# FFN up projection of a streaming encoder step: cache store, operand addresses, sample rounds and the order of the first pass

## The chip, the cores and the metric

The kernel runs on one core of one Trainium2 chip. The metric is the device time of one execution in microseconds (us). Three runs of the kernel before gave 1390.81, 1395.69 and 1397.09 us; the median, 1395.69 us, is its time. A further execution was profiled, and the profile is read from that one.

## The reference, cut to what matters

One layer: a mixer, a residual, then a feed-forward block whose up-projected rows go through a causal convolution of width 3 before the gated product.

```python
def conv_ffn(xn, buf, w_up, conv_w, conv_b, w_down):
    up = xn @ w_up                                   # (T, 1024) @ (1024, 5632)
    up, buf = causal_dwconv(up, buf, conv_w, conv_b) # buf: last 2 up-projected rows
    gate, val = jnp.split(up, 2, axis=-1)
    return (jax.nn.gelu(gate, approximate=True) * val) @ w_down, buf
...
x = x + rms_norm(h, g_mix_post[l])
h, ffn_buf = conv_ffn(rms_norm(x, g_ffn_pre[l]), ...)
x = x + rms_norm(h, g_ffn_post[l])
```

It is computed for a prompt of 1024 rows and for 32 sample rows that continue another stream. `ffn_buf`, the last two up-projected rows (2 x 5632 values), is an output for each of the two: `p_fc` and `q_fc`, both laid out 128 x 44 x 2.

## The kernel before, in words

The mixer and its output projection come first. `outproj` (L1074 on) handles units of 128 rows, 0 to 7, and unit 8, the sample rows: product with `w_out` (tiles zp), norm, residual, second norm, then eight transposes (tiles fxt, L1194) into features-first form. Units 0 to 4 and 8 are stored to `xn_d` and read back; units 5, 6 and 7 are written straight into the tiles x0 and xg1 (L1197 on ScalarE for unit 5, L1199 on VectorE for 6 and 7). Unit 7's norm is a chain over four engines: squares (L1159, ScalarE), sum and power (L1163, L208, L209, GpSimd), scaling (L1167, L1168, VectorE), squares (L1175), L208, L209, scaling (L1178), transposes, L1199.

**FFN up.** The product with `w_up` goes by Strassen-Winograd: seven products of quarter size in place of eight (p1 to p7). The output features are taken in NF = 22 blocks, `up_block` (L1309 on), each a pair of 128 gate and 128 value features. The moving operands are made once from the normed x by `col_operands` (L1227 on): B21, B11, T1, B22 and T2, T4, T3, each as a high and a low half of the fp32 value, so that one product of fp32 values is three matmuls (`mm3`, L88, L89, L90: high by high, high by low, low by high). Products p6, p4 and p7 use T2, T4 and T3. The stationary operands (A and S tiles) are halves of the block's weights, made by `up_operands`; the weights of block f + 1 are loaded (L1276, tiles wu) on SyncE's queue while block f runs. A block is 84 matmuls of 128x512.

Block 0 is cut in two, s = 0 and s = 1, each on 256 columns of every half of the prompt, because units 6 and 7 come late. In block 0, T2, T4 and T3 of s = 0 go into a pool px1 that lies where the output projection's weights lie until their last matmul. In `up_block` the bank of p6 is copied away (c6, L1329, ScalarE) before p7 adds to it.

**Order of the work.** The program is written as generators that are stepped by hand; a scheduler then fixes one static order for each engine, by emission order, priorities (`tc.high_priority`) and ordering hints (`tc.issue_after`). Each engine takes its instructions strictly in that order, and so does each queue: an instruction that waits holds all behind it. SyncE's queue carries the weight loads, the stores of finished blocks (h_d, L1407) and the sample weights.

**Sample rows.** `up_samples` (L1413 on) multiplies the 32 sample rows by `w_up` in fp32 in 24 rounds, (g, k) for three column groups and eight slices of 128 rows; each round uses one 1 MB buffer of two, and reloads it (L1418). `up_all` steps this generator between the two halves of a block. At its end the last two columns of `smp_u` are stored to `q_fc`: for each of 128 partitions 44 pieces of two values, 8 bytes each, from a row of 34 values.

**FFN down** (`down_all`) is also seven products (P2, P1, P4, P6, P5, P7, P3), each 11 steps of 12 matmuls, 132. Its stationary operands are halves of h (tag hop) in a pool ph that takes over the place of px0 (B21, B11, T1, B22); its moving operands are weight halves in p4.

**Addresses.** A pool lays its tiles end to end. By the tiles' sizes, B21, B11, T1, B22 and all weight halves in p4 start on multiples of 64 bytes. T2, T4 and T3 start 32 bytes past one, and so do h's halves (behind a 32-byte tile `pad` in ph). The output projection's two operands, both in p2, start 32 bytes past one as well.

Of the kernel before, what the change touches and what calls it, by code (L numbers as in the profile page):

```python
# [8 lines left out]
F32 = mybir.dt.float32  # L9
# [10 lines left out]
DEC = 32  # L20
# [58 lines left out]
def body(ctx: ExitStack, tc: tile.TileContext, a: dict):  # L79
# [988 lines left out]
    def outproj(p2, W, u):  # L1068
# [113 lines left out]
        if u < 5 or u == 8:  # L1182

            zt = z[:, :8 * n].rearrange("p (k n) -> p k n", n=n)
        else:
            s = u > 5
            o = 128 * (u - 4) - 256 * s
            zt = xlate[s][:, :, o:o + n]
        for hf in range(2):
            p, t, b = (upper[0], "xw", 4) if u == 5 else (upper[0], *(("xw", 4), ("sx", 1))[hf]) if 5 < u < 8 else (psb, "big", 3)  # L1190
            ps = p.tile([128, 4, 128], F32, tag=t, name=f"fxt{u}{hf}", bufs=b)
            for k in range(4):
                c = 512 * hf + 128 * k
                pe.transpose(ps[:, k, :n], z[:n, c:c + 128], ident[:n, :n])  # L1194
# [32 lines left out]
    def col_operands(pool_, q, s, between=lambda: None, res=None, only=False, c=slice(None), stages=(0, 1), begun=()):  # L1227

        res = {} if res is None else res
        q = {k: v[:, :, c] for k, v in q.items()}  # L1230
        at = slice(256 * s + (c.start or 0), 256 * s + (c.stop or 256))

        def halves(name, src):
            if name not in res:
                p = pool_[name in ("T2", "T4", "T3")]
                res[name] = tuple(p.tile([128, 4, 512], F32R, name=f"{name}{x}") for x in "hl")
            h, l = (t[:, :, at] for t in res[name])
            with ExitStack() as late:
                if s == 0 and name in ("B21", "B11"):
                    late.enter_context(tc.issue_after(kept["ch"].ins))  # L1240
                    late.enter_context(tc.issue_after(kept["cl"].ins))
                act.copy(h, src)
                return dve.tensor_tensor(l, src, h.bitcast(F32), op=ALU.subtract)

        if not begun:
            halves("B21", q["B21"])
            halves("B11", q["B11"])
        if only:
            return res
        t1 = q["B11"]  # L1250
        if 0 in stages:
            between()
            dve.tensor_tensor(t1, q["B12"], t1, op=ALU.subtract)
            halves("T1", t1)
            halves("B22", q["B22"])
        if 1 not in stages:
            return res
        t3, t2, t4 = q["B12"], q["B22"], q["B21"]
        dve.tensor_tensor(t3, q["B22"], t3, op=ALU.subtract)
        dve.tensor_tensor(t2, t2, t1, op=ALU.subtract)  # L1260
        dve.tensor_tensor(t4, t2, t4, op=ALU.subtract)
        with ExitStack() as behind:
            if s == 0:
                behind.enter_context(tc.issue_after(kept["jk"].ins))
            halves("T2", t2)
        ins = halves("T4", t4)
        between()
        with tc.issue_after(ins.ins):
            halves("T3", t3)
        return res  # L1270
# [45 lines left out]
    def up_block(pw_, f, s, W, X, uu, own={}):  # L1316
# [21 lines left out]

        y = bank(psb, "big", "puy", 3)
# [5 lines left out]
        if f == NF - 1:  # L1345
            prod(w, "p5", True, True)
            c5 = keep("c5", w)
            prod(x, "p1", True, True)
            c1 = keep("c1", x)
            out(0, 0, c1, y)  # L1350
            prod(w, "p3", False, True)
            yield
            prod(x, "p6", False, True)
            c6 = keep("c6", x)
            prod(z, "p4", True, True)
        elif f:
            prod(x, "p1", True, True)
            c1 = keep("c1", x)
            out(0, 0, c1, y)
            prod(w, "p5", True, True)  # L1360
            c5 = keep("c5", w)
            prod(z, "p4", True, True)
            yield
            prod(x, "p6", False, True)
            c6 = keep("c6", x)
            prod(w, "p3", False, True)
        else:

# [12 lines left out]
            c6 = keep("c6", x)  # L1381
            prod(z, "p4", True, True)
# [26 lines left out]
    def up_samples():  # L1409
# [19 lines left out]
        for g, (c0, nq) in enumerate(UGROUPS):  # L1429
            ps = psf.tile([128, 512], F32, tag="sx", name=f"us{g}", bufs=1)  # L1430
            for k in range(8):
# [4 lines left out]
                if k < 7:  # L1436
                    yield
# [9 lines left out]
        sp.dma_start(a["q_fc"], smp_u[:, :, DEC:DEC + 2])  # L1447
# [13 lines left out]
    def up_all(pw_, W0, X, uus, py, freed, ahead, begun):  # L1461
# [5 lines left out]
        for f in range(NF):  # L1467
# [3 lines left out]
            for s in (0, 1) if f == 0 else (None,):  # L1471
# [371 lines left out]
    blk = up_block(pw_, 0, 0, W0, X, uus[0], own)  # L1843
# [9 lines left out]
    sp.dma_start(fconv, a["fconv"])  # L1853
    uus[0] += [p7.tile([128, 2 + SEQ], F32, name=f"uu{j}") for j in range(2)]
# [14 lines left out]
    with tc.high_priority(offset=10 * AHEAD):  # L1869
        col_operands(px, q1, 1, res=X, only=True)  # L1870
# [19 lines left out]
    for i, _ in enumerate(up_all(pw_, W0, X, uus, lambda: py[0], freed, ahead, blk)):  # L1890
        if i == 1:

            for x, c in zip(last, (slice(0, 128), slice(128, 256))):
                with tc.issue_after(done[0].ins), tc.issue_after(kept["c6"].ins):
                    next(x)
                col_operands(px, q1, 1, res=X, c=c, stages=(0,), begun=True)
            col_operands(px, q1, 1, res=X, stages=(1,), begun=True)
# [4 lines left out]
    sp.dma_start(a["p_fc"], fhalo)  # L1902
    p9s.close()
# [142 lines left out]
```

## Time and profile before

| | |
|---|---|
| median of three runs | 1395.69 us |
| the profiled execution | 1403.19 us |
| its span, first to last instruction | 1401.4 us |
| around the span | 1.8 us |
| mean granted TensorE clock | 0.977 |
| TensorE (PE) busy | 1324.7 us, 95% |
| VectorE (DVE) busy | 1014.0 us, 72% |
| ScalarE (ACT) busy | 693.8 us, 50% |
| GpSimd (POOL) busy | 310.5 us, 22% |

All times in the rows are microseconds from the span's start. A row of the timeline has start, duration, engine, line, operation, out<-in, partitions and elements, and in brackets the idle time before it with what ended it. A matmul's duration is modelled and overlaps the next one, so its pace is read from the distance between starts. A row of the stage table has the stretch, its length, busy time and instruction count of PE, of its weight loads, of DVE, ACT and POOL, then the granted TensorE clock (1.00 is full), the mean busy share of the 16 DMA engines and the GB/s that they moved. FFN up runs from 661 to 1160 us, FFN down from there to 1392 us.

### The profile page before, as it was taken

The numbers are of one execution on the slowest core, as the hardware profiler recorded it, in microseconds if no ns is written. First come the engines' busy times: TensorE is split into PE (matmuls) and PEld (weight loads), VectorE is DVE, ScalarE is ACT, GpSimd is POOL, SyncE is SP. The second block draws the span as 40 slices with busy tenths as digits, with TensorE's granted clock in tenths as the row PEclk, the third lists the DMA queues.
The fourth block names the chain that finished last, engine by engine and source line by source line (L and its number), as shares of the span: only waits on it lengthen the run. The fifth ranks groups of instructions, "written<-read, shape, count | busy, mean of one in ns | idle before, by whom it ended". The sixth has DMA issues, their size and how long they took to land.

```text
span 1401.4 us, 25578 instructions
## 1 busy us (share of the span) xinstructions
PE 1324.7 (95%) x9896; PEld 1103.0 (79%) x9896; DVE 1014.0 (72%) x1748; ACT 693.8 (50%) x1294; POOL 310.5 (22%) x411
## 2 busy tenths in 40 slices
PE   7999999998989999999799999999994999999997
PEld 6999899997988978687677777777773777678885
DVE  5886569768697687846887777788772965499456
ACT  5546556445665455525454444445441544444552
POOL 4533212144122442321101102123013100010005
PEclk9999999999999999989899999999997999999999
DMA  9799879776899654434257878876759339644335
GB/s 342 242 342 359 281 229 310 236 268 199 280 292 340 215 189 160 150 120 152 77 184 209 239 194 227 226 194 198 199 148 38 89 131 354 262 156 142 124 111 120
DMA packets 140288, 291.73 MB, mean 208 GB/s; under 512 B 34519, under 2 KB 69495, under 8 KB 138039
## 3 DMA queue, kind: packets, MB, share of 16 engines
q1 hardware_dynamic: 126535, 267.03, 58.8%
q0 software_dynamic: 9120, 18.62, 7.4%
q10 hardware_dynamic: 4512, 4.46, 0.9%
q8 instruction: 77, 1.26, 0.4%
q14 instruction: 44, 0.36, 0.1%
HBM read 229.38 MB, written 85.78 MB: 225 GB/s over the span
## 4 chain that ended last, share of the span: by engine, by line
PE 57%; DVE 8%; DMA 7%; ACT 3%; issue 2%; POOL 1%; SPq 0%; DVEq 0%; POOLq 0%; ACTq 0%
PE pux_None L88 4%; PE pux_None L90 4%; PE pux_None L89 4%; PE q L88 3%; PE q L89 3%; PE q L90 3%; PE puw_None L89 3%; PE puw_None L88 3%; PE puw_None L90 3%; PE x L88 2%; DMA wu19r<-in_w_up 2%; PE x L89 2%; PE x L90 2%; PE us L1433 2%; PE zp L88 1%
## 5 line engine op out<-in xcount | busy, mean ns | idle before, releaser
L1403 DVE SCALAR_TENSOR_TENSOR y<-uu,fconv_sb,y 128x1024 f32<-128x1024 f32 x88 | 116.0, 1318 | 23.3 <-ACT y L1401 22.9
L1400 POOL COPY fhalo<-uu 128x2 f32<-128x2 f32 x44 | 17.7, 402 | 369.1 <-DVE uu L1334 369.1
L88 PE MATMUL pv<-wt_0h,xh 128*128 128x256 f32 (+1 forms) x192 | 55.8, 291 | 4.2 <-DVE xl L321 1.6
L90 PE MATMUL zp<-woh,cl 128*128 128x512 f32 (+1 forms) x144 | 57.9, 402 | 1.5 <-DVE cl L1093 1.5
L88 PE MATMUL zp<-woh,ch 128*128 128x512 f32 (+1 forms) x144 | 57.7, 410 | 0.7 <-ACT ch L1092 0.7
L89 PE MATMUL zp<-wol,ch 128*128 128x512 f32 (+1 forms) x144 | 58.1, 404 | 0.0
L1401 ACT ACTIVATE y<-uu,fconv_sb 128x1024 f32<-128x1024 f32 x44 | 54.8, 1245 | 6.3 <-DVE uu L1334 5.1
L90 PE MATMUL pv<-wt_1h,xl 128*128 128x256 f32 (+1 forms) x192 | 55.4, 289 | 0.0
L88 PE MATMUL pv<-wt_1h,xh 128*128 128x256 f32 (+1 forms) x192 | 54.9, 286 | 0.0
L89 PE MATMUL pv<-wt_1l,xh 128*128 128x256 f32 (+1 forms) x192 | 54.6, 284 | 0.0
L90 PE MATMUL pv<-wt_0h,xl 128*128 128x256 f32 (+1 forms) x192 | 54.4, 283 | 0.0
L89 PE MATMUL pv<-wt_0l,xh 128*128 128x256 f32 (+1 forms) x192 | 54.2, 282 | 0.0
L1636 POOL TENSOR_TENSOR gss<-gss 128x1 f32<-128x1 f32 (+1 forms) x9 | 8.0, 887 | 194.9 <-ACT gjk L1629 194.9
L208 POOL TENSOR_SCALAR hrs<-hss 128x5 f32<-128x5 f32 (+3 forms) x27 | 11.0, 408 | 177.8 <-DVE hss L1002 174.7
L818 DVE COPY_PREDICATED P<-masks_sb,sc 128x352 f32<-128x352 int32 (+3 forms) x53 | 37.8, 713 | 5.8 <-PE sc L731 5.2
L88 PEld LDWEIGHTS pv<-wt_0h,xh 128*128 128x128 f32 x192 | 35.9, 187 | 6.1 <-DVE xl L321 1.9
L1006 POOL TENSOR_TENSOR cat<-cat,gt 128x320 f32<-128x320 f32 (+3 forms) x27 | 31.3, 1160 | 26.1 <-DVE cat L1004 25.9
L88 PEld LDWEIGHTS pv<-wt_1h,xh 128*128 128x128 f32 x192 | 36.3, 189 | 0.7 <-issue 0.6
L209 POOL TENSOR_TENSOR hrs<-hrs,mhalf 128x5 f32<-128x5 f32 (+3 forms) x27 | 36.2, 1341 | 2.2
L90 PEld LDWEIGHTS pv<-wt_1h,xl 128*128 128x128 f32 x192 | 36.3, 189 | 0.3
L89 PEld LDWEIGHTS pv<-wt_1l,xh 128*128 128x128 f32 x192 | 36.3, 189 | 0.1
L89 PEld LDWEIGHTS pv<-wt_0l,xh 128*128 128x128 f32 x192 | 35.9, 187 | 0.2
(1881 smaller groups left out, 4684.7 us busy)
## 6 DMA issues: line engine op xcount, KB each, us to landing
wus<-in_w_us SPq DMA_DIRECT2D x16, 1024.0 KB, 7.8
wrP<-in_w_dn SPq DMA_DIRECT2D x27, 512.0 KB, 3.9
h_d<-y SPq DMA_DIRECT2D x22, 512.0 KB, 4.7
ht<-h_d SPq DMA_DIRECT2D x22, 512.0 KB, 9.9
wt_0r<-in_w_tok SPq DMA_DIRECT2D x21, 512.0 KB, 5.6
wt_1r<-in_w_tok SPq DMA_DIRECT2D x21, 512.0 KB, 6.4
ws_d<-in_w_dn POOLq DMA_DIRECT2D x20, 512.0 KB, 7.4
wrP<-ws_d SPq DMA_DIRECT2D x20, 512.0 KB, 3.8
```

Source lines behind the costliest of these rows:

```text
L88: pe.matmul(ps, lh[0], rh[0], start=first, stop=False, **kw)
L89: pe.matmul(ps, lh[0], rh[1], start=False, stop=False, **kw)
L90: return pe.matmul(ps, lh[1], rh[0], start=False, stop=last, **kw)
L208: pool.tensor_scalar(out, ss, 1.0 / width, eps, op0=ALU.mult, op1=ALU.add)
L209: pool.tensor_tensor(out, out, mhalf[:n, :cols], op=ALU.pow)
L818: dve.copy_predicated(dst, mk.broadcast_to([n, 11, *mk.shape[2:]]), src)
L1006: pool.tensor_tensor(cat[:n, c0:c0 + 64 * nh], cat[:n, c0:c0 + 64 * nh], gt[:n, c0:c0 + 64 * nh], op=ALU.mult)
L1400: behind["POOL"] = pool.tensor_copy(fhalo[:, j, :], u[:, SEQ - 2:SEQ])
L1401: act.activation(y, u, AF.Identity, scale=fconv[:, j, 2:3], bias=fconv[:, j, 3:4])
L1403: dve.scalar_tensor_tensor(y, uu[i][:, s:s + SEQ], fconv[:, j, s:s + 1], y, op0=ALU.mult, op1=ALU.add)
L1433: pe.matmul(ps[DEC * q:DEC * q + DEC], smp_x[:, k, :], wus[:, i % 2, q, :], start=k == 0, stop=k == 7)
L1636: pool.tensor_tensor(ss[:n, 0:1], ss[:n, 2:3], ss[:n, 3:4], op=ALU.add)
```

## The change

- **Cache.** The two columns are first copied on GpSimd into a packed tile `fcq`, and `fcq` is stored to `q_fc` after FFN up, behind the store of `p_fc`.
- **Addresses.** Two 32-byte tiles are put around x0, `fcq` takes 352 bytes; together T2, T4 and T3 move by 416 bytes, six and a half times 64. The 32-byte `pad` in ph goes, so h's halves move by 32 bytes.
- **Sample rounds.** The generator yields after every second round, and `up_all` steps it up to 15 times where it stepped it 28; the first step, which loads the sample cache (5632 pieces of 8 bytes) and the first two buffers, comes in block 2, not 1.
- **First pass.** `col_operands` is cut into parts: B (B21, B11), T (T1, B22), t (T2, T4), q (T3). Unit 5's transposes are kept in PSUM, and its eight scalings (L1197) are issued after B11's high half. T2 and T4 of s = 0 are written into the upper, not yet used columns of B22 and T1 (`early`), ahead of px1; four GpSimd copies of 128x1024 values take them to their place later. B21 and B11 of s = 1 are issued after T3.
- **Last block.** In block 21 the order is p5, p1, p2, p3, p6, p4, p7; it was p2, p5, p1, p3, p6, p4, p7.

```diff
@@ outproj
+        held = []
...
-            if 5 <= u < 8 and (u, hf) not in ((6, 0), (6, 1), (7, 0), (7, 1)):
-                for k in range(4 * hf, 4 * hf + 4):
-                    act.activation(zt[:, k, :], ps[:, k % 4, :], AF.Copy, scale=gcols[:, k:k + 1])
+            if u == 5:
+                held.append(ps)
                 continue
...
+        if u == 5:
+            yield
+            for k in range(8):
+                act.activation(zt[:, k, :], held[k // 4][:, k % 4, :], AF.Copy, scale=gcols[:, k:k + 1])
@@ col_operands
-    def col_operands(pool_, q, s, between=lambda: None, res=None, only=False, c=slice(None), stages=(0, 1), begun=()):
+    def col_operands(pool_, q, s, between=lambda: None, res=None, c=slice(None), parts="BTtq", at_=None):
...
+            if at_ and name in at_:
+                h, l = at_[name]
+            else:
...
+        if "q" in parts:
+            with tc.issue_after(kept["T4l"].ins), tc.issue_after(kept["T4"].ins), tc.issue_after(kept["T2"].ins):
+                halves("T3", t3)
@@ up_block
+        if f == NF - 1:
+            w = bank(psf, "xw", "puw", 4)
+            prod(w, "p5", True, True)
+            c5 = keep("c5", w)
+            yield
+            x = bank(psf, "xw", "pux", 4)
+            prod(x, "p1", True, True)
+            c1 = keep("c1", x)
+            y = bank(psb, "big", "puy", 3)
+            prod(y, "p2", True, True)
+            out(0, 0, c1, y)
+            prod(w, "p3", False, True)
+            yield
...
@@ up_samples
-                if k < 7:
+                if k in (1, 3, 5):
                     yield
...
-        sp.dma_start(a["q_fc"], smp_u[:, :, DEC:DEC + 2])
+        pool.tensor_copy(fcq, smp_u[:, :, DEC:DEC + 2])
@@ up_all
-                while f and n_rounds < f * 28 // 18:
+                while f and n_rounds < f * 15 // 17:
@@ body
+    p3.tile([128, 8], F32, name="pad0")
     x0 = p3.tile([128, 8, 2, 256], F32, tag="xg0", name="xg0", bufs=1)
+    p3.tile([128, 8], F32, name="pad2")
...
-    X = col_operands(px, q0, 0, lambda: next(ops), stages=(0,))
-    next(ops)
+    X = col_operands(px, q0, 0, parts="B")
+    with tc.issue_after(kept["B11"].ins):
+        next(firsts[-1])
+    col_operands(px, q0, 0, lambda: next(ops), res=X, parts="T")
+    early = {n: tuple(t[:, :, 256:] for t in X[m]) for n, m in (("T2", "B22"), ("T4", "T1"))}
+    col_operands(px, q0, 0, lambda: next(ops), res=X, parts="t", at_=early)
+    X0 = {**X, **early}
...
+    fcq = p7.tile([128, NU, 2], F32, name="fcq")
...
-    col_operands(px, q0, 0, res=X, stages=(1,), begun=True)
+    col_operands(px, q0, 0, res=X, parts="q")
+    X0["T3"] = X["T3"]
...
+    for n in ("T2", "T4"):
+        X[n] = tuple(px1.tile([128, 4, 512], F32R, name=f"{n}{x}") for x in "hl")
...
-    with tc.high_priority(offset=10 * AHEAD):
-        col_operands(px, q1, 1, res=X, only=True)
+    with tc.high_priority(offset=10 * AHEAD), tc.issue_after(kept["T3"].ins):
+        col_operands(px, q1, 1, res=X, parts="B")
...
-        ph[0].tile([128, 8], F32, name="pad")
...
         if i == 1:
+            for n in ("T2", "T4"):
+                for t, e in zip(X[n], early[n]):
+                    pool.tensor_copy(t[:, :, :256], e)
...
     sp.dma_start(a["p_fc"], fhalo)
+    sp.dma_start(a["q_fc"], fcq)
```

More of the change, by code (lines that the diff above doesn't have):

```diff
@@ L1233, in halves @@
         def halves(name, src):
[L1234 to L1237, printed above, removed]
+            if at_ and name in at_:
+                h, l = at_[name]
+            else:
+                if name not in res:
+                    p = pool_[name in ("T2", "T4", "T3")]
+                    res[name] = tuple(p.tile([128, 4, 512], F32R, name=f"{name}{x}") for x in "hl")
+                h, l = (t[:, :, at] for t in res[name])
             with ExitStack() as late:
@@ L1241, in halves @@
                     late.enter_context(tc.issue_after(kept["cl"].ins))
-                act.copy(h, src)
+                kept[name] = act.copy(h, src)
                 return dve.tensor_tensor(l, src, h.bitcast(F32), op=ALU.subtract)
[L1245 to L1251, printed above, removed]
+        t1, t2, t3, t4 = q["B11"], q["B22"], q["B12"], q["B21"]
+        if "B" in parts:
+            halves("B21", t4)
+            halves("B11", t1)
+        if "T" in parts:
             between()
-            dve.tensor_tensor(t1, q["B12"], t1, op=ALU.subtract)
+            dve.tensor_tensor(t1, t3, t1, op=ALU.subtract)
             halves("T1", t1)
[L1255 to L1269, printed above, removed]
+            halves("B22", t2)
+        if "t" in parts:
+            dve.tensor_tensor(t3, t2, t3, op=ALU.subtract)
+            dve.tensor_tensor(t2, t2, t1, op=ALU.subtract)
+            dve.tensor_tensor(t4, t2, t4, op=ALU.subtract)
+            with ExitStack() as behind:
+                if s == 0:
+                    behind.enter_context(tc.issue_after(kept["jk"].ins))
+                halves("T2", t2)
+            kept["T4l"] = halves("T4", t4)
+            between()
+        if "q" in parts:
+            with tc.issue_after(kept["T4l"].ins), tc.issue_after(kept["T4"].ins), tc.issue_after(kept["T2"].ins):
+                halves("T3", t3)
         return res
@@ L1337, in prod @@
             product(ps, p, W, X, first, last, at)
+        if f == NF - 1:
[11 more added lines that the diff above has]
+            yield
+            z = bank(psb, "big", "puz", 3)
+            prod(x, "p6", False, True)
+            c6 = keep("c6", x)
+            prod(z, "p4", True, True)
+            out(0, 1, c6, w)
+            yield
+            prod(x, "p7", False, True)
+            c7 = keep("c7", x)
+            out(1, 1, c5, x)
+            out(1, 0, c7, z, ALU.subtract)
+            yield
+            return
         y = bank(psb, "big", "puy", 3)
@@ L1344, in up_block @@
         z = bank(psb, "big", "puz", 3)
[L1345 to L1356, printed above, removed]
+        if f:
             prod(x, "p1", True, True)
```

6 lines of the change are left out of this document (3 added, 3 removed).

## The prediction

> **What bounds the kernel now.** I read the page first: the busy times, then the slices of the span.
>
> ```profile
> span 1401.4 us, 25578 instructions
> PE 1324.7 (95%) x9896; PEld 1103.0 (79%) x9896; DVE 1014.0 (72%) x1748; ACT 693.8 (50%) x1294; POOL 310.5 (22%) x411
> PE   7999999998989999999799999999994999999997
> ```
>
> TensorE is busy for 95% of the span, so the kernel is as long as TensorE's work plus its holes. One slice of 35 us has a 4 among nines (the 31st, about 1051 to 1086 us); the rest can come only from holes too small for a slice or from a better pace of the matmuls. The second view is the stage table.
>
> ```profile
> 661.20:710.10 48.90, 40.98 (x250) 35.34 (x248) 39.32 (x52) 25.93 (x40) 8.57 (x10) 0.90 0.36 106
> 710.10:1065.50 355.40, 355.40 (x1604) 272.19 (x1600) 277.84 (x340) 166.41 (x253) 61.29 (x70) 1.00 0.74 196
> 1065.50:1092.20 26.70, 5.26 (x14) 3.88 (x15) 5.64 (x5) 3.75 (x6) 2.59 (x2) 0.62 0.79 60
> 1128.00:1159.60 31.60, 29.42 (x122) 23.47 (x121) 19.55 (x25) 12.38 (x18) 1.38 (x3) 0.95 0.50 179
> 1159.60:1391.97 232.37, 230.51 (x1013) 174.12 (x1011) 152.76 (x241) 107.25 (x204) 26.12 (x34) 1.00 0.56 178
> ```
>
> FFN up from block 2 on (second row) and FFN down (last row) have TensorE busy throughout at a full clock: there only the pace counts. Three stretches have holes: the first pass (7.9 us idle, clock 0.90), 26.7 us in block 18 with 5.3 us of matmuls, and the last block (2.2 us idle). In the third row the DMA engines are 79% busy and move 60 GB/s, where the row above it moves 196 GB/s at 74%: many small pieces.
>
> **The cache store.** The timeline around the hole, SyncE first, then the start of product p3 (tile puw, operand B22) in blocks 17 to 20:
>
> ```profile
> 1051.91 0.65 SPq L1447 DMA_DIRECT2D out_q_fc<-smp_u  x1
> 1053.96 9.30 SPq L1276 DMA_DIRECT2D wu19r<-in_w_up  x1
> 1085.45 0.62 ACT L94 CAST A_19h<-wu19r 128x512 fp32r<-128x512 f32 x1 [25.11 <-DMA wu19r<-in_w_up]
> 1086.12 0.80 PE L88 MATMUL puy_None<-B21h,A_19h 128*128 128x512 f32 x1 [20.63 <-ACT A_19h L94]
> ...
> 1048.40 0.39 PE L88 MATMUL puw_None<-B22h,S_17h 128*128 128x512 f32 x1
> 1092.17 0.39 PE L88 MATMUL puw_None<-B22h,S_18h 128*128 128x512 f32 x1
> 1111.53 0.40 PE L88 MATMUL puw_None<-B22h,S_19h 128*128 128x512 f32 x1
> 1130.91 0.40 PE L88 MATMUL puw_None<-B22h,S_20h 128*128 128x512 f32 x1
> ```
>
> The store of 5632 pieces of 8 bytes goes out at 1051.91. The weight load behind it takes 9.30 us to be issued and is used only at 1085.45, 31.5 us after its issue began. ScalarE waits for it 25.11 us, TensorE 20.63 us. From B22 to B22 this block takes 43.77 us, the two after it 19.36 and 19.38: the loss is 24.4 us, with the slow matmuls after the hole. A few small transposes of the sample rows lie in it and stay, so I count 24. In the changed kernel the store has 128 pieces of 352 bytes and is issued after `p_fc`, when no up weight is left to load; the GpSimd copy that packs it is 128x88 values with nobody behind it but the sample rows' own products. Next in line is the weight load itself: by block 20's rows (B21 at 1108.50, below, 3.0 us ahead of B22) its first use was due at 1048.40 + 19.4 - 3.0 = 1064.8, 10.8 us after its issue; without the small pieces nothing of the hole should stay. Bounds: 20.6 (only TensorE's named wait) and 24.4.
>
> **Addresses.** Starts of consecutive products of 12 matmuls in block 18 to 19, of two successive products of FFN down (132 matmuls from start to start), and of two matmuls of the output projection with 17 intervals between them:
>
> ```profile
> 1097.41 0.40 PE L88 MATMUL pux_None<-T3h,S_18h 128*128 128x512 f32 x1
> 1100.22 0.40 PE L88 MATMUL pux_None<-B11h,A_19h 128*128 128x512 f32 x1
> 1102.97 0.39 PE L88 MATMUL puw_None<-T1h,S_19h 128*128 128x512 f32 x1
> 1105.69 0.40 PE L88 MATMUL puz_None<-T4h,A_19h 128*128 128x512 f32 x1
> 1108.50 0.40 PE L88 MATMUL puy_None<-B21h,A_20h 128*128 128x512 f32 x1
> ...
> 1330.20 0.40 PE L88 MATMUL x<-P7w,P7h 128*128 128x512 f32 x1
> 1361.00 0.40 PE L88 MATMUL q<-P3w,P3h 128*128 128x512 f32 x1
> ...
> 603.05 0.40 PE L88 MATMUL zp<-woh,ch 128*128 128x512 f32 x1
> 606.92 0.39 PE L90 MATMUL zp<-woh,cl 128*128 128x512 f32 x1
> ```
>
> T3 takes 2.81 us, B11 behind it 2.75, T1 2.72, T4 2.81. With the addresses that the tile sizes give, T3 and T4 start 32 bytes past a multiple of 64 while their stationary weights start on one; for B11 and T1 both start on one. In FFN down it is the stationary h that is 32 bytes past, and a matmul takes 30.80/132 = 0.2333 us, the pace of T3 and T4 (2.81/12 = 0.234), not that of T1 (0.2267). In the output projection both operands are 32 bytes past: 3.87/17 = 0.2276. So not the address by itself seems to cost, but that the two operands differ in it. The change puts T2, T4, T3 and h's halves on multiples of 64, and all pairs agree. A block of seven products at 2.72 is 19.04 us against 19.38: 0.34 over 21 blocks is 7.1 us; if the T products only come down to B11's 2.75, it is 3 x 0.06 x 21 = 3.8. I take 6, since B11 is slow only directly behind a T product. FFN down has 7 x 132 = 924 matmuls: at 0.2267 they gain 6.1 us, at 0.2276 5.3; I take 5.5. Both stages are TensorE-bound by the table, so it all counts.
>
> A rule of the Trainium skill speaks against these two terms: "SBUF — State Buffer", "Who interferes with whom", gives TensorE two independent read ports, one for the moving operand and one for weights, and says that it never waits on anyone. By it both terms would be 0; the rows above show a difference that it does not explain, though not its cause.
>
> **Sample rounds.** Starts of p3 again, with two rounds in the first interval and one in the second:
>
> ```profile
> 985.96 0.39 PE L88 MATMUL puw_None<-B22h,S_14h 128*128 128x512 f32 x1
> 1007.34 0.39 PE L88 MATMUL puw_None<-B22h,S_15h 128*128 128x512 f32 x1
> 1027.87 0.39 PE L88 MATMUL puw_None<-B22h,S_16h 128*128 128x512 f32 x1
> ```
>
> Against 19.38 without a round, one costs 20.53 - 19.38 = 1.15 us, two 21.38 - 19.38 = 2.00. A second round is 0.85, so a visit in itself is 0.30. By the step counts in the code (28 f // 18 gives blocks 1 to 17 one or two steps each) the 24 rounds went in 17 visits; in pairs they go in 12: 5 x 0.30 = 1.5 us. Each pair finds both buffers loaded a block earlier, as the two-round blocks did.
>
> **The first pass.** VectorE, GpSimd and ScalarE rows on its path and TensorE's waits, in time order; then two prices on GpSimd from the groups by form:
>
> ```profile
> 654.39 1.22 DVE L1243 TENSOR_TENSOR B21l<-xg,B21h 128x1024 fp32r<-128x1024 f32 x1 [8.25 <-ACT B21h L1242]
> 662.25 2.56 POOL L1163 TENSOR_TENSOR oss<-oss 128x1 f32<-128x1 f32 x1 [0.90 <-ACT c L1159]
> 670.41 0.38 PE L89 MATMUL pux<-T2l,S_0h 128*128 128x256 f32 x1 [3.16 <-DVE T2l L1243]
> 672.28 3.27 POOL L208 TENSOR_SCALAR oss<-oss 128x1 f32<-128x1 f32 x1 [5.61 <-ACT z L1175]
> 676.22 1.15 ACT L1178 ACTIVATE z<-xr,oss 128x1024 f32<-128x1024 f32 x1 [4.02 <-POOL oss L209]
> 677.68 0.39 PE L88 MATMUL pux<-T3h,S_0h 128*128 128x256 f32 x1 [2.65 <-ACT c L1329]
> 680.04 2.21 PE L1194 MATMUL fxt<-ident,z 128*128 128x128 f32 x12
> ...
> L97 POOL TENSOR_TENSOR wf_0l<-wf_0r,wf_0h 128x1024 fp32r<-128x1024 f32 x1 | 2.4, 2406 | 1.7 <-DVE wf_0h L96 1.7
> L224 POOL MEMSET kt<- 128x1024 f32 x1 | 0.9, 946 | 0.0
> ```
>
> VectorE idles 8.25 us before its first B operand and then has no time to spare: p6 waits 3.16 us for T2's low half. As p6 ends late, its copy c6 stands on ScalarE behind L1178, which waits for unit 7's GpSimd chain, and p7 waits 2.65 us for it; unit 7's transposes at 680.04 come behind that. With the change B21 and B11 (about 2.4 us of VectorE) go into the idle stretch, and T2 and T4 need not wait for px1's place, so both waits should go: 5.8 us. What is late next is unit 7's chain, which sets T1 of s = 1. On GpSimd four copies of 128x1024 are new. A memset of that size takes 0.95 us, an operation with two inputs 2.41; a copy reads one input, so about 1.7 each, 3.8 to 9.6 for four. Queued behind them may be L208 and L209 of unit 7, for which L1178, the transposes and the second pass wait; and T1 and B22 of s = 1 must wait until the copies have read. I charge one copy: 5.8 - 1.8 = 4 us. Bounds: all 7.9 us of idle time gone, or the four copies at 9.6 on the chain against 3.2 for T2, a loss of 6.4.
>
> The same page and section say that a GpSimd instruction that reads SBUF and a VectorE one with two SBUF inputs exclude each other for their whole length; L208 on one column, 3.27 us at 672.28, agrees. By it the copies would also hold VectorE, and the term would be its lower bound.
>
> The sample cache's load moves to block 2, beside weight loads; it was issued in the first row of the stage table, whose DMA share is 0.36, so I charge nothing for it. If it held the queue as the store did, it would cost the store's 24 us.
>
> **The last block.**
>
> ```profile
> 1153.99 0.62 ACT L94 CAST P2h<-ht 128x512 fp32r<-128x512 f32 x1 [8.70 <-DMA ht<-h_d]
> 1155.14 0.50 PE L88 MATMUL pux_None<-T3h,S_21h 128*128 128x512 f32 x1 [2.18 <-ACT c_21None L1329]
> 1159.57 0.63 PE L88 MATMUL q<-P2w,P2h 128*128 128x512 f32 x2
> ```
>
> c6 stood behind a cast that waited 8.70 us for a load; p7 lost 2.18 us, and then ran at 4.43 us instead of 2.81. Together 3.8 us. With p4 as cover between p6 and p7 the copy can stand ahead of that cast, but the order is the scheduler's, and P2 needs the load anyway. I take 2.5, bounds 0 and 3.8.
>
> **Sum.** 24 + 6 + 5.5 + 1.5 + 4 + 2.5 = 43.5 us. The profiled execution took 1403.2 us (1401.4 of span, 1.8 around), 7.5 above the median of the runs; it would come to 1359.7. Taken from the median, 1395.7 - 43.5 = 1352.2; I forecast 1352.
>
> **Rivals.** First, addresses do nothing, and the T products are slow for another reason, such as their banks: 11.5 us fall away, 1364. For it: products differ in bank too, and the rule above. Against: FFN down shows the same pace with other banks. Second, the four copies take GpSimd and VectorE in the first pass and its term falls to -6.4: 1362. For it: VectorE is busy for 39.3 of 48.9 us there. Third, the change does not do what it says: the hole is only moved, because the cache's load now meets the weight loads of block 3, or because the weight load was late for another reason: 1376. Against: in the stretch of the load TensorE's waits name other things. Fourth, on the other side: without its 20 us pause TensorE draws on for 690 us and its granted clock falls. From 661 to 1392 us there are 731 us, 688 after the gains; slower than before by over 0.5% (7 us) needs 688/c of 738, a clock below 0.932; at 0.93 the time is 1404. Against: 355 us on end at 1.00 in the table.
>
> **How the numbers follow.** The forecast has 0.55, the address rival 0.15, the copies 0.18, the moved hole 0.10, the clock 0.02. The runs of before lie 6.3 us apart, so 0.5% (7 us) is about what can be told from no change. Upper bounds of all terms (24.4, 7.1, 6.1, 1.5, 7.9, 3.8) sum to 50.8: 1345, and the spread of the runs (3 either way) makes it 1342. The high end takes in the first two rivals, and half of the moved hole, plus the spread: 1371. Every case but the last is faster by over 0.5%; the first three rivals together would leave 1398, within 0.5%, which I give 0.01. So faster 0.97, same 0.01, slower 0.02.
>
> **What would show it.** Right: no gap over 2 us on TensorE between 1050 and 1110 us, and p3 to p3 even there; the T products at 2.72 us and FFN down's products at 29.9 instead of 30.8; 12 visits of sample rounds; the T2l and c6 waits gone, the GpSimd copies done before T1 of s = 1 is written; no 2.18 us wait before P2. Wrong: a wait for a weight load in blocks 2 to 4 or 19; T products still at 2.81; L208 of unit 7 behind a copy, with TensorE waiting for T1 of s = 1 later than now.

## The result, and the profile after

The changed kernel takes 1362.86 us (median of 4 runs, 1360.69 to 1364.20), the kernel before on the same chip 1395.31 (1390.81 to 1397.09): a ratio of 0.9771, 95% interval 0.9743 to 0.9798, or 32.4 us. The forecast was 1352: the direction held, and so did most of the store's term and all of FFN down's; 11 us of the gain did not come. The profiled execution took 1360.69 us, 1358.9 of it span.

The page of the changed kernel, the slices of TensorE:

```profile
PE   6999999998999999999799999999999999999997
```

The 4 in the 31st slice is gone. The stage table again, over the first pass, from there to B22 of block 18, and over the last block with P2:

```profile
654.30:698.40 44.10, 37.07 (x233) 33.29 (x231) 40.14 (x52) 24.89 (x40) 11.56 (x15) 0.92 0.40 117
698.40:1057.30 358.90, 357.23 (x1630) 275.92 (x1630) 287.29 (x346) 170.55 (x259) 65.60 (x72) 1.00 0.70 198
...
1109.40:1155.70 46.30, 46.30 (x217) 33.43 (x216) 28.15 (x37) 20.18 (x33) 0.77 (x2) 1.00 0.95 352
```

The first pass still has 7.0 us of idle time, the second row, which had none, now has 1.7, and the last block, which had 2.2, has none. The timeline shows the store, on SyncE's queue, and p3's starts in blocks 16 to 19. As in the prediction, a block's time is taken from the B22 start of the block before it to its own:

```profile
1015.22 0.34 SPq L1935 DMA_DIRECT2D out_q_fc<-fcq  x1
...
1016.29 0.40 PE L88 MATMUL puw_None<-B22h,S_16h 128*128 128x512 f32 x1
1038.04 0.39 PE L88 MATMUL puw_None<-B22h,S_17h 128*128 128x512 f32 x1
1057.30 0.40 PE L88 MATMUL puw_None<-B22h,S_18h 128*128 128x512 f32 x1
1076.61 0.40 PE L88 MATMUL puw_None<-B22h,S_19h 128*128 128x512 f32 x1
```

Block 18 takes 19.26 us where it took 43.77. But block 17, which has no round of matmuls left in it, takes 21.75. And the products of block 18 to 19, to be laid beside those of the prediction:

```profile
1062.57 0.40 PE L88 MATMUL pux_None<-T3h,S_18h 128*128 128x512 f32 x1
1065.36 0.39 PE L88 MATMUL pux_None<-B11h,A_19h 128*128 128x512 f32 x1
1068.09 0.39 PE L88 MATMUL puw_None<-T1h,S_19h 128*128 128x512 f32 x1
1070.81 0.40 PE L88 MATMUL puz_None<-T4h,A_19h 128*128 128x512 f32 x1
1073.61 0.39 PE L88 MATMUL puy_None<-B21h,A_20h 128*128 128x512 f32 x1
...
1289.32 0.39 PE L88 MATMUL x<-P7w,P7h 128*128 128x512 f32 x1
1319.24 0.39 PE L88 MATMUL q<-P3w,P3h 128*128 128x512 f32 x1
```

T3 and T4 take 2.79 and 2.80 us (2.81 before): hardly anything moved. FFN down's product takes 29.92 us (30.80 before), just as forecast. One address term came whole, the other not.

### The profile page after: what moved, and what is told of

Same layout as the page of the kernel before. It is cut to its first block, busy times and chain, and to the rows that moved or that the text cites. A ratio compares the mean times of both kernels' runs of the same rounds, so it can differ in the third digit from the quotient of the medians.

```text
span 1358.9 us, 25577 instructions
## 1 busy us (share of the span) xinstructions
PE 1307.7 (96%) x9896; PEld 1097.5 (81%) x9896; DVE 1018.0 (75%) x1748; ACT 693.8 (51%) x1294; POOL 316.2 (23%) x416
## 4 chain that ended last, share of the span: by engine, by line
PE 57%; DVE 12%; ACT 3%; issue 2%; DMA 2%; POOL 1%; DVEq 0%; SPq 0%; POOLq 0%; ACTq 0%
PE pux_None L88 4%; PE pux_None L90 4%; PE pux_None L89 4%; PE puw_None L88 3%; PE puw_None L90 3%; PE puw_None L89 3%; PE q L88 2%; PE q L90 2%; PE q L89 2%; PE x L88 2%; PE x L89 2%; PE x L90 2%; PE us L1452 2%; PE zp L88 1%; PE zp L90 1%
## 5 line engine op out<-in xcount | busy, mean ns | idle before, releaser
L1422 DVE SCALAR_TENSOR_TENSOR y<-uu,fconv_sb,y 128x1024 f32<-128x1024 f32 x88 | 115.6, 1314 | 25.3 <-ACT y L1420 24.6
L208 POOL TENSOR_SCALAR hrs<-hss 128x5 f32<-128x5 f32 (+3 forms) x27 | 10.1, 374 | 174.2 <-DVE hss L1002 169.6
L1424 ACT ACTIVATE y<-y 128x1024 f32<-128x1024 f32 x22 | 23.3, 1059 | 27.7 <-DVE y L1422 27.7
L90 PEld LDWEIGHTS pv<-wt_0h,xl 128*128 128x128 f32 x192 | 36.4, 189 | 0.2
```

The costliest lines, as they stand in the source:

```text
L90: return pe.matmul(ps, lh[1], rh[0], start=False, stop=last, **kw)
L208: pool.tensor_scalar(out, ss, 1.0 / width, eps, op0=ALU.mult, op1=ALU.add)
L1422: dve.scalar_tensor_tensor(y, uu[i][:, s:s + SEQ], fconv[:, j, s:s + 1], y, op0=ALU.mult, op1=ALU.add)
L1424: act.activation(ys[0], ys[0], AF.Gelu_apprx_tanh)
```

## The experiments

Each ratio is to the kernel before on the same chip, with its 95% interval. Four groups follow: the addresses, the store, the new stall, the other edits.

### Addresses

The tile sizes give T2, T4 and T3 at 32 modulo 256 bytes in the kernel before and at 128 in the changed one; their stationary weights stand at 0 in both. FFN down's h went from 32 to 0, with moving weights at 0. So "on a multiple of 64" and "agreeing modulo 256" say the same of h and different things of T. First the pad under T2, T4 and T3 alone:

```diff
-    p7.tile([128, 8], F32, name="pad1")
+    p7.tile([128, 40], F32, name="pad1")
```

> The changed kernel with one edit: the pad below T2, T4 and T3 grows by 128 bytes, so that they lie at 0 modulo 256 like the stationary weights they are multiplied with (in the changed kernel they lie at 128, in the kernel before at 32). Theory A: the pace of a matmul follows whether its moving and its stationary operand agree modulo 256 bytes. Then the T2, T3 and T4 products fall from 2.79 to 2.72 us, a block without sample rounds from 19.31 to about 19.1, and the whole from 1362.9 to about 1358 (3 products x 0.07 x 21 blocks = 4.4 us, up to 5). Rival B: the T products are slower for their place in the block or their banks, and addresses do nothing: T3 stays at 2.79 and the time at 1363.

Ratio 0.9741 (0.9718 to 0.9765), 1354.69 us in the median of 6. The products:

```profile
1059.16 0.39 PE L88 MATMUL pux_None<-T3h,S_18h 128*128 128x512 f32 x1
1061.88 0.39 PE L88 MATMUL pux_None<-B11h,A_19h 128*128 128x512 f32 x1
1064.60 0.39 PE L88 MATMUL puw_None<-T1h,S_19h 128*128 128x512 f32 x1
```

T3 takes 2.72 us, and B11 behind it as well (2.73 in the changed kernel, 2.75 before). Same order, same banks, only an address: rival B is out. Next a pad under the split weights, which moves both partners:

```diff
     p4 = p4s.enter_context(tc.tile_pool(name="p4", ...))
+    p4.tile([128, 32], F32, name="pad4")
```

> The changed kernel with one edit: a pad of 128 bytes below the tiles of the split weights, which moves the stationary weights of FFN up, its B operands, and both operands of FFN down from 0 to 128 modulo 256; T2, T4, T3 stay at 128. No operand is then on a multiple of 256, but all pairs agree. Theory A (agreement counts): T products at 2.72, B products at 2.72 to 2.75 and FFN down's products at 29.9 as they are, about 1358 us. Rival C (each operand has to start on a multiple of 256): every product of FFN up at 2.79 and of FFN down at 30.8, about 1363 + 4 x 0.07 x 21 + 6 = 1375. Rival B (addresses do nothing): 1363.

Ratio 0.9752 (0.9730 to 0.9774). The same view:

```profile
1058.78 0.39 PE L88 MATMUL pux_None<-T3h,S_18h 128*128 128x512 f32 x1
1061.50 0.39 PE L88 MATMUL pux_None<-B11h,A_19h 128*128 128x512 f32 x1
```

2.72 us again for T3, with no operand on a multiple of 256: the agreement of the two counts, not the place of either. Rival C is out. Then other differences, T by 64 and h by 128:

```diff
-    p7.tile([128, 8], F32, name="pad1")
+    p7.tile([128, 24], F32, name="pad1")
...
+        ph[0].tile([128, 32], F32, name="pad")
```

> The changed kernel with two edits: T2, T4, T3 moved from 128 to 64 modulo 256 (their stationary weights stay at 0), and FFN down's h halves (stationary) from 0 to 128 (its moving weights stay at 0). All stay on multiples of 64. The prediction's reading (a multiple of 64 is enough): FFN down's products stay at 29.9 us and the time at 1363 or below. Theory A (agreement modulo 256): T products at 2.79 to 2.80, FFN down's products back to 30.6 to 30.8, and the time near 1363 + 6 x 0.8 = 1368. A pace that depends on the size of the difference would show as T and h products that differ (64 against 128).

Ratio 0.9826 (0.9800 to 0.9852), 0.0055 or about 7.7 us above the changed kernel, with all operands on multiples of 64:

```profile
1063.86 0.40 PE L88 MATMUL pux_None<-T3h,S_18h 128*128 128x512 f32 x1
1066.62 0.40 PE L88 MATMUL pux_None<-B11h,A_19h 128*128 128x512 f32 x1
...
1292.01 0.40 PE L88 MATMUL x<-P7w,P7h 128*128 128x512 f32 x1
1322.81 0.40 PE L88 MATMUL q<-P3w,P3h 128*128 128x512 f32 x1
```

FFN down is back at 30.80 us a product, so a multiple of 64 is not enough. The T3 product is 2.76. So a difference of 0 gives 2.72, 64 gives 2.76, 128 gives 2.79, 32 gives 2.81; any difference tried here costs, though not in the order of its size. Last, h moved in the kernel before, and nothing else:

```diff
-        ph[0].tile([128, 8], F32, name="pad")
```

> The kernel before with the pad of 32 bytes under FFN down's h halves taken away and nothing else, so that they lie at 0 modulo 256 like the weights they meet. Theory (agreement): the products P5, P7 and P3 go from 30.80 to 29.92 us, 7 x 0.88 = 6.2 us less in all, or 5.5 if P1 and P2 keep stalls of their own: ratio 0.9956 to 0.996. Rival (addresses do nothing): 1.0.

Ratio 0.9956 (0.9939 to 0.9973), 6.1 us by the median of the chip, and P7 to P3 takes 29.92 us there too (1318.73 to 1348.65). The term of 5.5 stands by itself.

### The store

The packed store in the kernel before; the second pad keeps the old addresses:

```diff
+    fcq = p7.tile([128, NU, 2], F32, name="fcq")
+    p7.tile([128, 40], F32, name="pad3")
...
-        sp.dma_start(a["q_fc"], smp_u[:, :, DEC:DEC + 2])
+        pool.tensor_copy(fcq, smp_u[:, :, DEC:DEC + 2])
...
     sp.dma_start(a["p_fc"], fhalo)
+    sp.dma_start(a["q_fc"], fcq)
```

> The kernel before with the cache store alone changed: GpSimd packs the two columns, and they are stored in 128 pieces after p_fc; all operands keep their old addresses. The prediction's term: the hole of block 18 goes, 24 us, so 1395.3 - 24 = 1371. Theory now: the hole goes, but the sample rows' GpSimd chain, which ran inside it, comes out of its shadow and delays VectorE's splits of the next block by about 2 us as in the changed kernel: 1373. Rival: without the profiler the hole is shorter than the profile showed, and the store is worth less than 20: 1376 or more.

Ratio 0.9882 (0.9861 to 0.9902): 16.5 us, not 22 to 24. Its profile has the hole gone, with block 18 at 19.97 us (the pad keeps the 32 bytes, so nothing else should move):

```profile
1042.14 0.34 SPq L1905 DMA_DIRECT2D out_q_fc<-fcq  x1
1044.07 0.33 SPq L1276 DMA_DIRECT2D wu19r<-in_w_up  x1
...
1038.30 0.39 PE L88 MATMUL puw_None<-B22h,S_17h 128*128 128x512 f32 x1
1058.27 0.40 PE L88 MATMUL puw_None<-B22h,S_18h 128*128 128x512 f32 x1
```

The load behind the store, at the same place in the queue, is issued in 0.33 us instead of 9.30: the pieces did it. The delay of 2 us that I expected from the sample rows' GpSimd operations, now without the hole, did not come: they run from 1042 to 1059 us here, TensorE shows no wait there, and 19.97 is 0.6 above the 19.38 of the blocks behind it. To see why the medians differ less than the profiles (1401.4 against 1369.0 us of span), I took a second profile of the kernel before.

> The kernel before, unchanged, for a second profile. The packed store alone brought 16.5 us between medians, but its profile is 32.4 us shorter than the first profile of before, and the hole by itself 23.8. Theory: the first profile of before was a long draw (its stage ahead of FFN up took 661 us where all others take 654 to 656), so this one has a span near 1390, that stage at 654 to 656 and the hole about as long as before (B22 to B22 of block 18 at 41 to 44 us). Rival: the hole itself varies between executions and is shorter here, 36 to 40 us from B22 to B22, which would make the store worth about 17.

Its span is 1389.9 us, 11.5 below the first. The load behind the store, the cast that waits for it, and p3:

```profile
1046.13 8.96 SPq L1276 DMA_DIRECT2D wu19r<-in_w_up  x1
1074.69 0.62 ACT L94 CAST A_19h<-wu19r 128x512 fp32r<-128x512 f32 x1 [22.16 <-DMA wu19r<-in_w_up]
...
1040.57 0.39 PE L88 MATMUL puw_None<-B22h,S_17h 128*128 128x512 f32 x1
1081.32 0.39 PE L88 MATMUL puw_None<-B22h,S_18h 128*128 128x512 f32 x1
```

The hole is there, but block 18 takes 40.75 us, 3.0 less than in the first profile. Both theories had a part: the stage ahead of FFN up took 661.2 us in the first and 657.7 here, and the first pass to block 2 72.9 and 68.6. Against this second profile the packed store is worth 40.75 - 19.97 = 20.8 us in its block. The medians say 16.5 (13.6 to 19.3); in the one profile of the packed version the first pass and the last block took 3.6 us more than in the second of before, which would leave 17.2. The same two stretches differ by 6.5 us between the two profiles of the unchanged kernel, so whether the 4 us are chance or follow from the store is open.

### The stall of block 17

TensorE waits twice between 1000 and 1110 us in the changed kernel. Its timeline, VectorE and GpSimd first, then the link between them and TensorE, on ScalarE:

```profile
1029.15 2.74 DVE L1422 SCALAR_TENSOR_TENSOR y<-uu,fconv_sb,y 128x1024 f32<-128x1024 f32 x1
1026.10 2.57 POOL L1474 TENSOR_TENSOR smp_y<-smp_y,smp_y 128x704 f32<-128x704 f32 x1
1031.92 1.06 ACT L1424 ACTIVATE y<-y 128x1024 f32<-128x1024 f32 x1 [5.65 <-DVE y L1422]
1032.88 0.60 ACT L94 CAST A_18h<-wu18r 128x512 fp32r<-128x512 f32 x1
1033.54 0.50 PE L88 MATMUL puy_None<-B21h,A_18h 128*128 128x512 f32 x1 [0.55 <-ACT A_18h L94]
1035.15 0.51 PE L88 MATMUL pux_None<-T2h,S_17h 128*128 128x512 f32 x1 [1.12 <-ACT c_17None L1333]
```

The sample rows' convolution runs on GpSimd (L1470 to L1476); it is called the chain from here on. Beside it VectorE's L1422 takes 2.74 us. ScalarE's gelu (L1424) waits 5.65 us for that L1422, and the cast of A_18h, which TensorE needs, stands behind the gelu. In the first profile of the kernel before, the same chain ran from 1052 to 1064 us, just ahead of TensorE's long wait (1065.5 to 1086.1). VectorE's operation took 2.43 us beside it there too, but TensorE had no wait before the load's; nor had it in the version with the packed store, where there is no hole. So it is not the hole that hid the chain; the experiment old_steps below shows what did. I tried to cut it in steps, on the version with T at 0:

```diff
                 pool.tensor_tensor(dst, dst, smp_y[1], op=ALU.add)
+            yield
```

> The version with T at 0 (1354.7, ratio 0.9741), and the sample rows' GpSimd chain cut in three steps, of six, six and two operations, which the block loop then takes in blocks 17, 19 and 20 instead of all in 17. Theory: the new stall of 2.3 us in block 17 (TensorE waits for splits that VectorE makes at half speed beside the GpSimd chain) goes, as six slow operations are covered by the buffers: B22 to B22 of block 17 from 21.7 to 19.4 to 19.8, 1352.5 in all (ratio 0.9725). Rival: the stall comes from the transposes and ScalarE's copies of the sample rows, not from the chain: 21.7 stays and the time too. Other rival: each step stalls its own block by about 1 us, and the sum is the same.

Ratio 0.9709 (0.9683 to 0.9735), but block 17 takes 21.79 us: the chain ran at the same places as without the edit, since nothing on GpSimd held the later steps back. The edit did nothing, and the run is a second measurement of the version with T at 0. The stage ahead of FFN up took 651 us in its profile, 656 in the other: 0.3% between such measurements is chance. Then each step was held behind a copy of its block on GpSimd:

```diff
             for s in range(2):
+                if (lo > 0) != (s > 0):
+                    yield
+                with tc.issue_after(behind["POOL"].ins):
                     pool.tensor_tensor(smp_y[1], smp_u[:, js, s:s + DEC], w[s], op=ALU.mult)
                 pool.tensor_tensor(dst, dst, smp_y[1], op=ALU.add)
+        yield
```

> The version with T at 0 (ratio 0.9741), with the sample rows' GpSimd chain cut in steps of which each is also held behind the fhalo copy of its block on GpSimd (the cut alone had moved nothing: the chain ran at the same times). About six operations run in block 17 and five to seven two blocks later. Theory: the stall of block 17 comes from VectorE at half speed beside 16 us of chain, which holds y, then ScalarE's gelu, and behind it the cast that TensorE waits for; cut in two it is covered: B22 to B22 of block 17 from 21.7 to 19.4 to 20.2, later blocks 19.0 to 19.5, about 1353 in all, ratio 0.9728. Rival: the transposes and copies of the sample rows make the stall, 21.7 stays. Other rival: the two parts each stall their block, and the sum stays at 1354.7.

Ratio 0.9737 (0.9707 to 0.9767). The chain is cut now, and the profile's p3 starts of blocks 16, 17, 19 and 20 are

```profile
1016.25 0.39 PE L88 MATMUL puw_None<-B22h,S_16h 128*128 128x512 f32 x1
1036.12 0.39 PE L88 MATMUL puw_None<-B22h,S_17h 128*128 128x512 f32 x1
...
1074.19 0.39 PE L88 MATMUL puw_None<-B22h,S_19h 128*128 128x512 f32 x1
1094.35 0.39 PE L88 MATMUL puw_None<-B22h,S_20h 128*128 128x512 f32 x1
```

Block 17 falls to 19.87 us and block 20 rises to 20.16: of 1.9 us won 1.1 come back, so 0.7 stay, less than these medians can tell. To show the cause, the chain was left out (the sample rows' outputs are then not the reference's):

```diff
-            pool.tensor_tensor(dst, smp_u[:, js, 2:2 + DEC], w[2], op=ALU.mult)
...
+            act.copy(dst, smp_u[:, js, 2:2 + DEC])
```

> The version with T at 0, with the twelve GpSimd operations of the sample rows' convolution left out (two ScalarE copies stand in their place; the sample rows' outputs are then not the reference's). Theory: B22 to B22 of block 17 falls from 21.72 to 19.4 (19.04 and 0.4 for the transposes), and VectorE's operations there take 0.69 and 1.28 us instead of up to 2.7. Rival (transposes and ScalarE's copies make the stall): 21 or more.

```profile
1015.28 0.39 PE L88 MATMUL puw_None<-B22h,S_16h 128*128 128x512 f32 x1
1034.55 0.39 PE L88 MATMUL puw_None<-B22h,S_17h 128*128 128x512 f32 x1
...
1022.70 1.28 DVE L1422 SCALAR_TENSOR_TENSOR y<-uu,fconv_sb,y 128x1024 f32<-128x1024 f32 x1
```

Block 17 takes 19.27 us without the chain, against 21.72 with it in the version with T at 0, and L1422 takes 1.28. The chain costs 21.72 - 19.27 = 2.45 us; the transposes and copies that stayed cost 0.2. This is read from the block alone: the one execution without the chain took 1354.02 us, within the 1348.86 to 1358.80 of the version that has it.

### The other edits

The sample rounds stepped as before, in the changed kernel:

```diff
-                if k in (1, 3, 5):
+                if k < 7:
...
-                while f and n_rounds < f * 15 // 17:
+                while f and n_rounds < f * 28 // 18:
```

> The changed kernel with the sample rounds stepped as before (one or two a block). The prediction's term: 1.5 us more, 1364.4. Theory from the profiles: blocks 3 to 17 hold 23.8 us above the pace of a block without rounds in the kernel before, and 23.7 in the changed one when its stall of 2.3 is taken off, so the pairs brought at most 0.5: 1363 to 1363.4, ratio 0.977 to 0.9775, which a time of this spread can't tell from 1.5; the intervals can: they should sum to 313.5 to 316 from B22 of block 2 to B22 of block 17, against 315.6.

Ratio 0.9767 (0.9738 to 0.9796), the same as with pairs. By p3's starts, from block 2 to block 18 it takes 1062.99 - 728.81 = 334.2 us, the changed kernel 1057.30 - 722.45 = 334.9. With the old steps blocks 17 and 18 (20.50 and 19.95 us) hold hardly a stall, though there is no hole here either. The profile's p3 starts of blocks 17 and 18:

```profile
1043.04 0.40 PE L88 MATMUL puw_None<-B22h,S_17h 128*128 128x512 f32 x1
1062.99 0.40 PE L88 MATMUL puw_None<-B22h,S_18h 128*128 128x512 f32 x1
```

The chain, with the copy that packs the cache ahead of it, starts at another place: at 1046.63 us, 3.6 behind such a start, where with pairs it starts at 1014.42, 1.9 ahead of one. If the stall of 2.45 is taken off the changed kernel, and 0.2 off this one (19.95 less 19.3 and the 0.4 that the transposes cost in blocks 7 and 12), the pairs save 1.5 us: the forecast term, and less than the stall that they brought. The last block in its old order, in the changed kernel:

```diff
-        if f == NF - 1:
-            w = bank(psf, "xw", "puw", 4)
-            prod(w, "p5", True, True)
...
```

> The changed kernel with the last block in its old order. Theory: the new order brought 2.5 us (the prediction's term) to 4: from B22 of block 18 to the first P1 product 101 to 102.5 us instead of 98.4, the wait of 1.5 to 2.2 us ahead of P2 back, 1365.5 to 1367, ratio 0.979. Rival (the load sets the time in both): 98.4 and 0.977.

Ratio 0.9783 (0.9756 to 0.9810), 1.7 us by the medians, intervals overlapping. The profiles, from B22 of block 18 to P1, first with the old order, then in the changed kernel:

```profile
1060.71 0.40 PE L88 MATMUL puw_None<-B22h,S_18h 128*128 128x512 f32 x1
1123.52 0.50 PE L88 MATMUL pux_None<-T3h,S_21h 128*128 128x512 f32 x1 [2.20 <-ACT c_21None L1333]
1161.58 0.39 PE L88 MATMUL x<-P1w,P1h 128*128 128x512 f32 x1
```

```profile
1117.74 0.86 PE L88 MATMUL q<-P2w,P2h 128*128 128x512 f32 x3
1155.71 0.39 PE L88 MATMUL x<-P1w,P1h 128*128 128x512 f32 x1
```

100.9 and 98.4 us: 2.5. In the changed order P2's first matmuls stand ahead of p7 and cover c6.

The version called no_first_pass is the kernel before with all edits but the first pass: no GpSimd copies, T2 and T4 in px1 from the start, unit 5's scaling in its old place.

> The changed kernel with the first pass as it was before (its operands formed in the old order, T2 and T4 in px1 from the start, no GpSimd copies, unit 5's scaling in the old place); store, samples, last block and addresses as in the changed kernel. Theory: the first pass brought 2 to 3 us (the profiles give 72.9 and 70.1 us from its first matmul to B22 of block 2 without the edit, 68.1 with it), since the T2 wait of 3.2 us went but a wait of 3.3 for unit 7's z came: 1365 to 1366, ratio 0.979. The prediction's term of 4: 1367, 0.980. Rival (nothing gained): 1363, 0.977.

Ratio 0.9791 (0.9768 to 0.9814), 2.8 us above the changed kernel, intervals overlapping. From the first matmul of FFN up to B22 of block 2 the profiles with the old first pass give 72.9, 68.6, 71.5, 70.0 and 70.0 us (mean 70.6), those with the new one and T at 128 68.1, 66.7 and 66.6 (67.1): 3 to 3.5 us, where the first group spreads over 4.3 and the second over 1.5.

## Why the prediction was right or wrong

**Where the 31 us of the profiles lie.** Taken by stretches, from the second profile of before to the one after: ahead of FFN up 657.7 to 654.3, the first pass to block 2 68.6 to 68.1, blocks 3 to 17 314.3 to 315.6, block 18 40.7 to 19.3, from there to P1 101.0 to 98.4, FFN down 207.6 to 203.2: -3.3 - 0.5 + 1.3 - 21.5 - 2.6 - 4.4 = -31.0. The first of these is not the change's: nearly the same code took 651 to 662 us there in different executions. Of the 11 us that did not come, about 3 lie in the size of the store's hole, 4.6 in the T operands, 2.5 in the new stall and 1 in the first pass.

**T operands: the step that failed.** The prediction read rightly that what costs is that "the two operands differ"; it then took 64 bytes as the period ("puts T2, T4, T3 and h's halves on multiples of 64, and all pairs agree"). By it T operands and weights agree; modulo 256 they differ by 128, and 128 costs 2.79 us a product, nearly what 32 did. The rows quoted there could not tell: 0 against 32 fits any period above 32. Of the 6 us came about 1.4 (19.38 to 19.31 a block over 20 blocks). Moved 128 bytes on, the block falls to 1072.99 - 1053.95 = 19.04 us, the very number worked out in the prediction, 0.27 x 20 = 5.4 us more. The Trainium skill's page "SBUF — State Buffer", section "Who interferes with whom", which makes TensorE's two reads independent, would give 0 for both address terms; it does not explain that a pad alone takes 12 matmuls from 2.79 to 2.72 us.

**The store.** Gone as forecast and by the mechanism named, but sized in a long execution: 24.4 us in the first profile of before, 21.4 in the second. I subtracted the 24 of an execution 7.5 us above the median from the median itself; that mixes two bases, and 3 us of the miss lie there; the medians of the store alone make the term smaller still, 16.5. One detail failed: the store is not "issued after p_fc": it goes out at 1015.22 us, ahead of the loads of block 18, and harms nothing, because it has 128 pieces.

**The new stall, not in the sum.** 2.45 us, shown by leaving the chain out. Of the pairs the prediction counted the visits saved, and put at nothing what they do to the GpSimd operations behind the last round: with pairs these run where they hold the next block's splits, while with the old steps, hole or no hole, they cost a few tenths. VectorE's operations there take twice their time beside GpSimd's; the rule that the prediction quotes from the Trainium skill, the same page and section (a VectorE instruction with two SBUF inputs and a GpSimd one that reads SBUF exclude each other), was weighed for the first pass and held here: L1422 2.74 us beside the chain, 1.28 without.

**FFN down.** Right in mechanism and size: 29.92 us a product, 6.1 us in the run with that edit alone. The profile after shows only 4.4 us less from P1 on, since P1 took 43.26 us to P4 in that execution and 41.7 in all but one of the other profiles with this h.

**Samples, last block.** The pairs save 1.5 us and the last block 2.5, both as forecast. By the step counts the rounds went in 16 visits, not 17, since block 1's step only loads: the sum should have held 4 x 0.30 = 1.2. And the pairs moved the GpSimd chain to where it stalls, so that together with the stall they lose 0.7.

**The first pass.** About 3 of 4 us. The waits for T2l and c6 went. The four GpSimd copies take 6.7 us, as estimated, and are done long before T1 of s = 1 is written at 672.01, but something else is late next, as this view of the changed kernel shows (two splits on VectorE, beside the copies and behind them, come first):

```profile
663.85 2.05 DVE L1250 TENSOR_TENSOR T3l<-xg,T3h 128x1024 fp32r<-128x1024 f32 x1
667.80 1.21 DVE L1250 TENSOR_TENSOR B11l<-xg,B11h 128x1024 fp32r<-128x1024 f32 x1
664.78 2.02 POOL L1924 CAST T4l<-T1l 128x1024 fp32r<-128x1024 f32 x1
668.01 1.41 POOL L209 TENSOR_TENSOR oss<-oss,mhalf 128x1 f32<-128x1 f32 x1
670.97 0.62 ACT L1249 CAST B22h<-xg 128x512 fp32r<-128x512 f32 x1 [5.57 <-DVE xg L1199]
672.79 1.15 ACT L1178 ACTIVATE z<-xr,oss 128x1024 f32<-128x1024 f32 x1
673.99 1.09 PE L1195 MATMUL fxt<-ident,z 128*128 128x128 f32 x8 [3.29 <-ACT z L1178]
```

L208 of unit 7 is behind the last copy, as feared, but its chain ends at 669.42, 3.4 us before z starts. z stands behind casts of s = 1 on ScalarE, the first of which waits 5.57 us for VectorE. So the new wait of 3.29 us comes from the order on ScalarE, and takes most of what T2's wait of 3.16 gave. VectorE is late there in part because of the copies: three of its splits (T1l, T3l, B21l) take 2.05 us each beside them instead of 1.22, 2.5 us in all. So the second rival's mechanism acts too, far below its price; how much of the 3.29 us is its part, no run here separates.

**The rivals.** Addresses as a whole do something, so the first rival is out. Its 1364 us lie nearer to the measured 1362.86 than the forecast does, but that is chance: 4.6 of its 11.5 us did not come, and the rest of the miss has other causes. The hole was not moved to another load. The clock did not fall: 0.984 to 0.989 in the runs after against 0.976 to 0.983 before.

**A better version** is the changed kernel with T at 0 modulo 256: 0.9741 and 0.9709 in its two measurements against 0.9771 (0.9743 to 0.9798). The stretches show the gain, 5.4 us of blocks 1 to 20; of the times alone, the interval of the first measurement (0.9718 to 0.9765) overlaps that of the changed kernel, and that of the second (0.9683 to 0.9735) does not.

## What to carry to other kernels

When steps of work are grouped, ask where all that stands behind the last of them will run, and beside what on the other engines. When a term is read from one execution, take it from the same base as the number it is subtracted from, or profile the kernel twice. And when a pace depends on an address, one good and one bad address leave the period open: compare with a third before choosing a pad.

## What the runs showed of the hardware

TensorE's pace for 128x512 matmuls depends on whether its moving and its stationary operand agree modulo 256 bytes. Agreeing at 0 or at 128 they start every 0.2267 us (29.92/132); with a difference of 32 or 128 between h and its weights every 0.2333 (30.80/132), and with 64 on the T operands at 0.230 (2.76/12). That neither operand's own place matters was the surprise: a pad under one pool helps or harms the products with a tile of another pool. Differences of 32, 64 and 128 all cost, so 256 is the least period that fits; no run was made to tell it from a longer one.

A store of 5632 pieces of 8 bytes kept the load behind it from being used for 31.5 us after its issue in one profile and 28.6 in the other; as 128 pieces of 352 bytes it leaves the next load's issue at 0.33 us.
